# Attention scores of two heads on the two halves of the tensor engine's rows, with three products of parts

## The chip, the cores and the metric

One core of a Trainium2 chip runs the whole program. The metric is the device time of one execution in microseconds; several executions are timed and their median is given. Engines are called as in the profile: PE (TensorE, matmuls) and PEld (its loads of weights), DVE (VectorE), ACT (ScalarE), POOL (GpSimd), SP (SyncE, which issues most DMAs).

## What is computed

The reference is an encoder of two layers in float32 over 512 tokens and 1024 channels. Each layer has a mixer (windowed attention beside a gated short convolution) and a gated feed-forward network. The change lies in the scores of the attention. Cut to that part:

```python
N_HEADS, HEAD_DIM, N_KV_HEADS, GROUP, BLOCK, WINDOW = 16, 64, 4, 4, 128, 128

def one_block(args):
    qi, ki, vi, mi = args          # 128 queries, the three key blocks around them
    sc = jnp.einsum('bqkgd,bskd->bkgqs', qi.astype(jnp.float32), ki.astype(jnp.float32)) * scale
    sc = jnp.where(mi[None, None, None], sc, NEG_INF)
    m = jnp.maximum(jnp.max(sc, axis=-1, keepdims=True), sink_f)
    p = jnp.exp(sc - m)
    denom = jnp.sum(p, axis=-1, keepdims=True) + jnp.exp(sink_f - m)
    o = jnp.einsum('bkgqs,bskd->bqkgd', p / denom, vi.astype(jnp.float32))
    return o.astype(qi.dtype)
```

A score is a dot product over the 64 channels of a head. Four query heads share a key head. Tokens come in four blocks of 128; a query block sees its own key block and its neighbours, so the first and the last see two blocks (256 keys) and the two in the middle three (384 keys).

## The kernel before

All operands of a matmul are in the type fp32r, which keeps fewer bits than float32. So that little is lost, each operand is split into a high part, the value rounded to fp32r, and a low part, the rest. A projection (`mm3`, lines 182 to 184) adds up three products of parts: high by low, low by high, high by high. `split_to` (lines 213 and 214) makes the parts: one copy on ACT, one subtraction on DVE. A tile `u` from `unit` holds both parts of 128 rows by 512 tokens.

Activations lie transposed, channels on the 128 partitions and tokens along the free axis. `query_tile(n)` projects two query heads at a time: partitions 0 to 63 (`lo_p`) hold head 2n, partitions 64 to 127 (`hi_p`) head 2n + 1; `rope` rotates them on DVE. Then, in lines 685 to 687, the kernel before doesn't put high parts in one half of the tile and low parts in the other. For each of the two heads it writes a plane of 128 rows: the head's own 64 rows get its high part (ACT, line 686) and the other 64 rows its low part (DVE, line 687). `key_tile` writes, for each key head, a tile whose plane 0 is the high part on both halves of the partitions and whose plane 1 is the low part on both halves.

So one matmul over 128 rows adds two products of parts at once, and `scores` (line 708) needs two matmuls per head: against the low part of the keys and against the high part, all four products of parts together. The weights (the stationary operand) are 128 queries of a head, the moving operand 256 or 384 keys, and the sum lies in a PSUM bank of its own, which DVE reads on line 713 (scale, mask, maximum).

The unit of work is a key head `g` with a query block `b`: 16 units per layer. `scores(at, 0)` does heads 0 and 1 of the group, `scores(at, 2)` heads 2 and 3, so there are two blocks of four matmuls per unit and 64 blocks in the program. `softmax` follows on ACT and DVE, then `weights` (four transposes, line 742, and a split) and `values` (line 755) per key block. The generator `products` yields after every three matmuls of a projection, and the loop over `pieces` strews the attention's pieces among these projections: a block of scores comes after a few projections or right after the four transposes, and projections follow it. PE takes its instructions in this order. `bank` hands out eight PSUM banks in turn.

One more matmul matters for the prediction: on line 124, early in the program, the 48 rows of convolution taps are transposed by a matmul on 48 rows. All other matmuls of the kernel before have 128 rows.

Of the kernel before, what the change touches and what calls it, by code (L numbers as in the profile page):

```python
# [10 lines left out]
F32 = mybir.dt.float32  # L11
# [3 lines left out]
ALU = mybir.AluOpType  # L15

P = 128
# [51 lines left out]
def encoder(ctx: ExitStack, tc: tile.TileContext, a, out):  # L69
    nc = tc.nc  # L70
# [14 lines left out]
    def nm(s):  # L85
        names[s] = names.get(s, -1) + 1
        return f"{s}_{names[s]}"

    def bank():
        return pp.tile([P, 512], F32, tag="bank", name=nm("bank"))  # L90

    def unit(shape, dtype=F32R):
        return up.tile(shape, dtype, tag="u4", bufs=22, name=nm("u4"))

    def t4(shape, dtype=F32):
        return sp.tile(shape, dtype, tag="t4", bufs=6, name=nm("t4"))
# [4 lines left out]
    def small(n, s="sm"):  # L101
        return sp.tile([P, n], F32, tag=s, bufs=4, name=nm(s))
# [83 lines left out]
    def gemm_steps(w, c0, xs):  # L186

        hl = w_cols(w, c0)
        acc = bank()
        for k in range(KT):  # L190
            mm3(acc, hl(0, k), hl(1, k), xs(k, 0), xs(k, 1), k == 0, k == KT - 1)
            yield
        return acc
# [18 lines left out]
    def split_to(h, lo, src):  # L212
        nc.scalar.copy(h, src)
        nc.vector.tensor_tensor(out=lo, in0=src, in1=h.bitcast(F32), op=ALU.subtract)  # L214
# [346 lines left out]
    g = t4([P, D])  # L561
# [5 lines left out]
    for l in range(DEPTH):  # L567
# [4 lines left out]
        def rope(acc):  # L572
            r1, r2 = t2([P, T]), t2([P, T])
            nc.vector.stream_shuffle(r2, acc, SWAP)
            nc.vector.tensor_tensor(out=r1, in0=acc, in1=cos, op=ALU.mult)
            nc.vector.tensor_tensor(out=r2, in0=r2, in1=sin, op=ALU.mult)
            nc.vector.tensor_tensor(out=r1, in0=r1, in1=r2, op=ALU.add)
            return r1

        lo_p, hi_p = slice(0, HD), slice(HD, P)  # L580
        kk = []
# [97 lines left out]
        qs = [None] * KT  # L679

        def query_tile(n):
            acc = yield from gemm_steps(w_in, Q0 + n * P, xs)
            qr = rope(acc)
            u = unit([P, 2, T])
            for i, (own, other) in enumerate(((lo_p, hi_p), (hi_p, lo_p))):
                nc.scalar.copy(u[own, i], qr[own])
                nc.vector.tensor_tensor(out=u[other, i], in0=qr[own], in1=u[own, i].bitcast(F32), op=ALU.subtract)
            qs[n] = u


        def blocks(b):
            return max(b - 1, 0), min(b + 1, NT - 1)

        def scores(at, i0):
            g, b = at["unit"]
            lo_b, hi_b = blocks(b)
            w = (hi_b - lo_b + 1) * P
            m0 = (lo_b - (b - 1)) * P
            if i0 == 0:
                at["m"] = small(GROUP, "m")  # L700
                at["p"] = []
            ps = t4([P, 2, 3 * P])
            m = at["m"]
            for i in (i0, i0 + 1):
                s = bank()
                q = qs[2 * g + i // 2][:, i % 2, b * P : (b + 1) * P]
                for part in range(2):
                    nc.tensor.matmul(  # L708
                        s[:, :w], q, kk[g][:, 1 - part, lo_b * P : lo_b * P + w], start=part == 0, stop=part == 1
                    )  # L710
                h = l * HEADS + GROUP * g + i
                p = ps[:, i % 2, :w]
                nc.vector.tensor_tensor_reduce(  # L713
                    out=p, in0=s[:, :w], in1=mask[:, m0 : m0 + w], scale=HD**-0.5,
                    scalar=sink[:, h : h + 1], op0=ALU.add, op1=ALU.max, accum_out=m[:, i : i + 1],
                )
                at["p"].append(p)
# [97 lines left out]
        def products():  # L815
            for c in range(KT):
                if 2 + c < KT:
                    yield from query_tile(2 + c)
                for i in range(3):
                    yield from conv_job(c, i)  # L820
            for m in range(KT):
                yield from conv_proj(m)


        units = [{"unit": (g, b)} for g in range(KV) for b in range(NT)]
        pieces = [[lambda: scores(units[0], 0)], [lambda: (scores(units[0], 2), softmax(units[0]))], [], [], []]
        behind = None
        for i, at in enumerate(units):
            lo_b, hi_b = blocks(at["unit"][1])
            ahead = units[i + 1] if i + 1 < len(units) else None  # L830
            for n in range(hi_b - lo_b + 1):
                first, second = [], []
                if behind:
                    second.append(lambda f=behind: values(*f))
                if ahead and n == 0:
                    first.append(lambda ahead=ahead: scores(ahead, 0))
                second.append(lambda at=at, n=n: weights(at, n))
                if ahead and n == 0:
                    second.append(lambda ahead=ahead: (scores(ahead, 2), softmax(ahead)))
                pieces += [first, second]  # L840
                behind = (at, n)
        pieces += [[], [lambda: values(*behind)]]

        for n in range(2):
            run(query_tile(n))
# [184 lines left out]
```

## Time and profile before

| | |
|---|---|
| median of 3 runs | 1653.22 us (1651.73 to 1653.52) |
| the profiled execution | 1652.12 us |
| its span, first to last instruction | 1650.3 us |
| PE busy | 1638.5 us, 10071 matmuls |
| PEld busy | 1473.4 us, 10071 loads |
| DVE, ACT busy | 1226.6 us, 936.1 us |
| matmuls of scores (line 708) | 256: 128 with 256 keys, 128 with 384 keys |

The busy time of an engine is the time in which at least one of its instructions runs. Matmuls overlap: the record of one with 512 columns is 0.39 us long while the next starts after 0.23 us. What a matmul costs in a stream is therefore read from start to start. Each matmul has a load of its weights (LDWEIGHTS, on PEld), which normally begins when the matmul before it starts. In a row of the timeline the columns are start, length, engine, line, operation, output and inputs, shape and count; several equal instructions in a row are merged.

### The profile page before, as it was taken

Reading aid. Unit: us, or ns where it says so; the run is one execution under the profiler, and the core shown is the slowest. Engines: PE = TensorE matmul, PEld = TensorE weight load, DVE = VectorE, ACT = ScalarE, POOL = GpSimd, SP = SyncE. Lnnn points to the kernel's source line nnn. Section 1 sums busy time; section 2 is a strip of 40 time slices with the busy share of each in tenths; the row PEclk is TensorE's granted clock in tenths of the full one; section 3 lists DMA queues with packets and bytes.
Section 4 is the critical chain, followed back from the end, with each engine's and each line's share of the span. In section 5 each row is a group of like instructions: output and inputs, shape, how many; then the busy total and the mean of one; then the engine's idle time right before and its main releaser. Section 6 shows DMA issues by size and latency. Waiting matters only on the chain.

```text
span 1650.3 us, 26580 instructions
## 1 busy us (share of the span) xinstructions
PE 1638.5 (99%) x10071; PEld 1473.4 (89%) x10071; DVE 1226.6 (74%) x2383; ACT 936.1 (57%) x1974; POOL 98.8 (6%) x146
## 2 busy tenths in 40 slices
PE   9999999999999999999999999999999999999998
PEld 8888888889989999988898888888998899999886
DVE  6988876649779988854469788766696898888442
ACT  5566666547657555553346676664576665556331
POOL 0000000000012100000000000000010211001000
PEclk9999999999999999999999999999999999999999
DMA  6322222345575334343423222223357643443332
GB/s 210 90 77 77 64 81 73 89 116 128 173 204 97 104 104 113 109 136 130 151 65 102 77 77 77 77 67 89 102 145 215 165 105 108 109 110 121 103 115 77
DMA packets 254625, 182.84 MB, mean 111 GB/s; under 512 B 6000, under 2 KB 237472, under 8 KB 254496
## 3 DMA queue, kind: packets, MB, share of 16 engines
q1 hardware_dynamic: 246240, 171.70, 35.3%
q0 software_dynamic: 7680, 8.39, 3.4%
q8 instruction: 79, 1.29, 0.3%
q10 hardware_dynamic: 576, 1.05, 0.2%
q14 instruction: 50, 0.41, 0.1%
HBM read 164.34 MB, written 8.39 MB: 105 GB/s over the span
## 4 chain that ended last, share of the span: by engine, by line
PE 66%; DVE 2%; DMA 1%; issue 1%; ACT 0%; POOL 0%; SPq 0%; POOLq 0%; DVEq 0%; ACTq 0%
PE bank L182 21%; PE bank L183 21%; PE bank L184 21%; PE bank L708 1%; PE bank L755 1%; DMA u<-in_w_up_dram 1%; PE bank L742 1%; DVE hl L132 1%; DVE t L441 0%; PE bank L373 0%; PE bank L251 0%; DVE t L271 0%; ACT t L235 0%; DVE h L214 0%; DVE t L243 0%
## 5 line engine op out<-in xcount | busy, mean ns | idle before, releaser
L182 PE MATMUL bank<-h,hl 128*128 128x256 f32 (+1 forms) x1536 | 494.1, 322 | 1.9 <-DVE h L214 1.9
L183 PE MATMUL bank<-h,hl 128*128 128x256 f32 (+1 forms) x1536 | 490.2, 319 | 0.0
L184 PE MATMUL bank<-h,hl 128*128 128x256 f32 (+1 forms) x1536 | 490.1, 319 | 0.0
L132 DVE TENSOR_TENSOR hl<-raw,hl 128x512 fp32r<-128x512 f32 x396 | 269.4, 691 | 169.7 <-ACT hl L131 168.2
L131 ACT CAST hl<-raw 128x512 fp32r<-128x512 f32 x396 | 241.7, 620 | 262.4 <-PE bank L184 221.3
L184 PEld LDWEIGHTS bank<-h,hl 128*128 128x128 f32 x1536 | 292.6, 190 | 20.8
L182 PEld LDWEIGHTS bank<-h,hl 128*128 128x128 f32 x1536 | 292.7, 191 | 20.6 <-DVE h L214 2.8
L183 PEld LDWEIGHTS bank<-h,hl 128*128 128x128 f32 x1536 | 292.8, 191 | 17.5
L182 PE MATMUL bank<-u,hl 128*128 128x256 f32 (+1 forms) x976 | 305.2, 313 | 0.6 <-DVE t L497 0.6
L184 PE MATMUL bank<-u,hl 128*128 128x256 f32 (+1 forms) x976 | 303.7, 311 | 0.0
L183 PE MATMUL bank<-u,hl 128*128 128x256 f32 (+1 forms) x976 | 303.6, 311 | 0.0
L132 DVE TENSOR_TENSOR hl<-t,hl 128x512 fp32r<-128x512 f32 x240 | 180.7, 759 | 22.4 <-ACT hl L131 20.9
L182 PEld LDWEIGHTS bank<-u,hl 128*128 128x128 f32 x976 | 186.2, 191 | 11.2 <-DVE t L497 1.4
L184 PEld LDWEIGHTS bank<-u,hl 128*128 128x128 f32 x976 | 186.2, 191 | 10.3
L183 PEld LDWEIGHTS bank<-u,hl 128*128 128x128 f32 x976 | 186.3, 191 | 9.5
L131 ACT CAST hl<-t 128x512 fp32r<-128x512 f32 x240 | 147.3, 620 | 67.4 <-DVE t L441 41.9
L182 PE MATMUL bank<-hl,u 128*128 128x512 f32 x304 | 118.3, 389 | 0.0
L183 PE MATMUL bank<-hl,u 128*128 128x512 f32 x304 | 118.3, 389 | 0.0
L184 PE MATMUL bank<-hl,u 128*128 128x512 f32 x304 | 118.3, 389 | 0.0
L728 ACT ACTIVATE t<-t,neg 128x256 f32<-128x256 f32 (+1 forms) x128 | 70.4, 552 | 21.1 <-DVE neg L723 20.8
L441 DVE TENSOR_TENSOR t<-t,raw 128x512 f32<-128x512 f32 x112 | 75.3, 683 | 1.0
L713 DVE CUSTOM_DVE_ANT_0 t<-bank,tab,sink 128x256 f32<-128x256 f32 (+1 forms) x128 | 65.7, 542 | 6.1 <-PE bank L708 5.9
(142 smaller groups left out, 2280.0 us busy)
## 6 DMA issues: line engine op xcount, KB each, us to landing
raw<-in_w_in_dram SPq DMA_DIRECT2D x88, 512.0 KB, 3.9
u<-in_w_up_dram SPq DMA_DIRECT2D x44, 512.0 KB, 6.4
raw<-in_w_down_dram SPq DMA_DIRECT2D x44, 512.0 KB, 3.6
raw<-in_w_gate_dram SPq DMA_DIRECT2D x40, 512.0 KB, 4.1
raw<-in_w_conv_proj_dram SPq DMA_DIRECT2D x16, 512.0 KB, 3.6
raw<-in_w_attn_proj_dram SPq DMA_DIRECT2D x16, 512.0 KB, 3.6
u<-in_w_in_dram SPq DMA_DIRECT2D x16, 512.0 KB, 5.7
raw<-in_w_out_dram SPq DMA_DIRECT2D x16, 512.0 KB, 4.1
```

The source lines that it names most:

```text
L131: nc.scalar.copy(h, raw)
L132: eng.tensor_tensor(out=lo, in0=raw, in1=h.bitcast(F32), op=ALU.subtract)
L182: nc.tensor.matmul(acc, wh, xl, start=first, stop=False, skip_group_check=goes_on)
L183: nc.tensor.matmul(acc, wl, xh, start=False, stop=False, skip_group_check=goes_on)
L184: nc.tensor.matmul(acc, wh, xh, start=False, stop=last, skip_group_check=goes_on)
L441: add = lambda out, x, y: nc.vector.tensor_tensor(out=out, in0=x, in1=y, op=ALU.add)
L708: nc.tensor.matmul(s[:, :w], q, kk[g][:, 1 - part, lo_b * P : lo_b * P + w], start=part == 0, stop=part == 1)
L713: nc.vector.tensor_tensor_reduce(out=p, in0=s[:, :w], in1=mask[:, m0 : m0 + w], scale=HD**-0.5, scalar=sink[:, h : h + 1], op0=ALU.add, op ...
L728: nc.scalar.activation(p, p, AF.Exp, bias=neg[:, i : i + 1], accum_out=den[:, i : i + 1])
L742: nc.tensor.transpose(pt[:, i * P : (i + 1) * P], p[:, n * P : (n + 1) * P], ident)
L755: nc.tensor.matmul(o, v, hl[:, 1 - part], start=n == 0 and part == 0, stop=kb == hi_b and part == 1)
```

## The change

`query_tile` now splits both heads of a tile with one call of `split_to`: plane 0 holds the high parts of both heads on their own rows, plane 1 the low parts. `scores` takes two banks first and then goes through three products of parts: low queries by high keys, high by low, high by high. For each product it issues one matmul for the lower head on partitions 0 to 63 and one for the upper head on partitions 64 to 127. Each has 64 rows and 128 columns of weights. The product of the two low parts is no longer computed.

```diff
             acc = yield from gemm_steps(w_in, Q0 + n * P, xs)
             qr = rope(acc)
             u = unit([P, 2, T])
-            for i, (own, other) in enumerate(((lo_p, hi_p), (hi_p, lo_p))):
-                nc.scalar.copy(u[own, i], qr[own])
-                nc.vector.tensor_tensor(out=u[other, i], in0=qr[own], in1=u[own, i].bitcast(F32), op=ALU.subtract)
+            split_to(u[:, 0], u[:, 1], qr)
             qs[n] = u
...
             ps = t4([P, 2, 3 * P])
             m = at["m"]
-            for i in (i0, i0 + 1):
-                s = bank()
-                q = qs[2 * g + i // 2][:, i % 2, b * P : (b + 1) * P]
-                for part in range(2):
+
+            q = qs[2 * g + i0 // 2]
+            sums = [bank() for _ in range(2)]
+            for n, (a_part, b_part) in enumerate(((1, 0), (0, 1), (0, 0))):
+                for s, rows in zip(sums, (lo_p, hi_p)):
                     nc.tensor.matmul(
-                        s[:, :w], q, kk[g][:, 1 - part, lo_b * P : lo_b * P + w], start=part == 0, stop=part == 1
+                        s[:, :w], q[rows, a_part, b * P : (b + 1) * P], kk[g][rows, b_part, lo_b * P : lo_b * P + w],
+                        start=n == 0, stop=n == 2,
                     )
+            for i, s in zip((i0, i0 + 1), sums):
                 h = l * HEADS + GROUP * g + i
                 p = ps[:, i % 2, :w]
                 nc.vector.tensor_tensor_reduce(
```

Line 708 of the kernel before is line 707 of the changed one; lines after the scores move by one.

On PE the first block of scores, between two steps of a projection, reads in the kernel before (`u_2_480` holds the keys, `u_6_545` the queries; the shape is that of the output):

```order
L183 MATMUL bank_646<-h_86,hl_640 128x512
L184 MATMUL bank_646<-h_86,hl_640 128x512
L708 MATMUL bank_661<-u_2_480,u_6_545 128x256 x2
L708 MATMUL bank_665<-u_2_480,u_6_545 128x256 x2
L182 MATMUL bank_646<-h_86,hl_643 128x512
```

At the same place of the changed kernel:

```order
L183 MATMUL bank_640<-h_86,hl_634 128x512
L184 MATMUL bank_640<-h_86,hl_634 128x512
L707 MATMUL bank_655<-u_2_480,u_6_545 128x256
L707 MATMUL bank_656<-u_2_480,u_6_545 128x256
L707 MATMUL bank_655<-u_2_480,u_6_545 128x256
L707 MATMUL bank_656<-u_2_480,u_6_545 128x256
L707 MATMUL bank_655<-u_2_480,u_6_545 128x256
L707 MATMUL bank_656<-u_2_480,u_6_545 128x256
L182 MATMUL bank_640<-h_86,hl_637 128x512
```

Two pairs, each into one bank, have become six single matmuls that alternate between two banks. All 64 blocks change in this way, and every other matmul of PE keeps its place in the stream.

On DVE the two subtractions of a query tile, on 64 partitions each, stand in the kernel before like this, with the first reads of scores (line 713) behind the third tile's projection (`bank_602`):

```order
L687 TENSOR_TENSOR u_7_589<-t_10_583,u_7_589 64x512 x2
L574 STREAM_SHUFFLE t_13_628<-bank_602 128x512
L575 TENSOR_TENSOR t_12_627<-bank_602,tab 128x512
L576 TENSOR_TENSOR t_13_628<-t_13_628,tab 128x512
L713 ISA t_5_660,m_659<-bank_661,tab,sink 128x256
L713 ISA m_659 128x1
L577 TENSOR_TENSOR t_12_627<-t_12_627,t_13_628 128x512
L713 ISA t_5_660,m_659<-bank_665,tab,sink 128x256
```

In the changed kernel:

```order
L214 TENSOR_TENSOR u_7_587<-t_10_581,u_7_587 128x512
L574 STREAM_SHUFFLE t_13_624<-bank_598 128x512
L575 TENSOR_TENSOR t_12_623<-bank_598,tab 128x512
L576 TENSOR_TENSOR t_13_624<-t_13_624,tab 128x512
L132 TENSOR_TENSOR hl_753<-raw_748,hl_753 128x512
L577 TENSOR_TENSOR t_12_623<-t_12_623,t_13_624 128x512
L714 ISA t_5_654,m_653<-bank_655,tab,sink 128x256
L714 ISA m_653 128x1
L714 ISA t_5_654,m_653<-bank_656,tab,sink 128x256
```

One subtraction has taken the place of two, and the two reads of scores, which stood on either side of line 577's addition, now follow each other behind it.

## The prediction

> **What bounds the kernel now.** The page comes first: the share of busy time by engine, and the clock that the tensor engine was granted.
>
> ```profile
> span 1650.3 us, 26580 instructions
> ...
> PE 1638.5 (99%) x10071; PEld 1473.4 (89%) x10071; DVE 1226.6 (74%) x2383; ACT 936.1 (57%) x1974; POOL 98.8 (6%) x146
> ...
> PEclk9999999999999999999999999999999999999999
> ```
>
> PE holds a matmul in 99% of the span and its clock is full in every slice. A busy PE need not be a fast PE, since the ends of matmuls are modelled, so I read all its costs from one start to the next. The view of waits, for PE alone, is the second:
>
> ```profile
> PE bank L182 <- DVE h L214: 1.9, 2, 1.4
> PE bank L620 <- POOL ident masks.py:199: 1.4, 1, 1.4
> PE bank L251 <- DVE t L239: 1.2, 1, 1.2
> PE bank L182 <- DVE t L497: 0.6, 1, 0.6
> PE bank L183 <- DVE h L214: 0.5, 1, 0.5
> ```
>
> PE waits 5.6 us in all for other engines, and none of these waits is at a score, a transpose of weights or a value product. So the stage that the change touches is bound by PE's own stream: time that it gains or loses there goes to the span one for one. What the scores take comes from the groups of line 708 (shapes kept apart) and from the timeline of PE around one block of each width; the second column is the length, the first the start.
>
> ```profile
> L708 PE MATMUL bank<-u,u 128*128 128x384 f32 x128 | 29.0, 348 | 0.0
> ...
> L708 PE MATMUL bank<-u,u 128*128 128x256 f32 x128 | 21.5, 290 | 0.0
> ```
>
> ```profile
> 56.98 0.39 PE L184 MATMUL bank<-h,hl 128*128 128x512 f32 x1
> 57.20 0.64 PE L708 MATMUL bank<-u,u 128*128 128x256 f32 x4
> 57.67 0.40 PE L182 MATMUL bank<-h,hl 128*128 128x512 f32 x1
> ```
>
> ```profile
> 81.94 0.39 PE L184 MATMUL bank<-h,hl 128*128 128x512 f32 x1
> 82.16 0.87 PE L708 MATMUL bank<-u,u 128*128 128x384 f32 x4
> 82.87 0.40 PE L182 MATMUL bank<-h,hl 128*128 128x512 f32 x1
> ```
>
> 128 matmuls of each width in blocks of four are 32 blocks of each. A block of width 256 takes 57.67 - 57.20 = 0.47 us (0.12 a matmul), one of width 384 takes 82.87 - 82.16 = 0.71 us (0.18 a matmul). All scores together: 32 x (0.47 + 0.71) = 37.8 us, 2.3% of the span. That is all there is to save or multiply.
>
> **The change, part by part.**
>
> *Six matmuls for four.* Each block now has six matmuls on 64 rows instead of four on 128. Two neighbours use different halves of the array's rows, different banks, and neither needs the other. No row of this trace has two matmuls on separate rows, so the price is bounded from both sides. Lower end: the two halves run side by side and a block lasts three steps, 3 x 0.12 = 0.36 and 3 x 0.18 = 0.53 us; 32 x (0.11 + 0.18) = 9.3 us are gained. Upper end: they run one after the other, six steps, 0.71 and 1.07 us; 32 x (0.24 + 0.36) = 18.9 us (unrounded steps) are lost. I take the lower end: no wait, operand or bank joins the two, and what the trace shows of the array in one place speaks for it, since a weight load begins while the matmul before it still streams. But it is a choice, and both ends stay. The Trainium skill, "TensorE: Matmul & The Clock Gate", Part 3, says that matmuls on distinct row groups run concurrently and start some 4 ns apart; by that the sum would be the gain of 9.3 us, and no run here shows it yet.
>
> *The change of tile shape.* Every block now lies between matmuls on 128 rows. The program before does this once: the transpose of the conv taps on line 124 has 48 rows. It stands in the timeline of PE, and of the weight loads (PEld) for the same stretch:
>
> ```profile
> 31.76 0.28 PE L183 MATMUL bank<-hl,h 128*128 128x256 f32 x1
> 31.88 0.28 PE L184 MATMUL bank<-hl,h 128*128 128x256 f32 x1
> 32.09 0.26 PE L124 MATMUL bank<-ident,cw_rows 48*128 48x48 f32 x1
> 32.28 0.38 PE L182 MATMUL bank<-h,hl 128*128 128x256 f32 x1
> 32.50 0.28 PE L183 MATMUL bank<-h,hl 128*128 128x256 f32 x1
> ```
>
> ```profile
> 31.76 0.19 PEld L184 LDWEIGHTS bank<-hl,h 128*128 128x128 f32 x1
> 32.09 0.14 PEld L124 LDWEIGHTS bank<-ident,cw_rows 48*128 48x128 f32 x1
> 32.28 0.19 PEld L182 LDWEIGHTS bank<-h,hl 128*128 128x128 f32 x1
> 32.38 0.19 PEld L183 LDWEIGHTS bank<-h,hl 128*128 128x128 f32 x1
> ```
>
> Elsewhere the weights of a matmul are loaded one step ahead, when the one before it starts. Here neither L124's load nor the next L182's is early: each begins with its own matmul, after a gap. From L184's start at 31.88 to L183's at 32.50 are 0.62 us; L184 and L182 at their usual step (31.76 to 31.88) are 0.24 of it, so this trip to another shape cost 0.38 us, its one small matmul in it. The comparison is a trip to transposes of full size, eight in a row:
>
> ```profile
> 25.13 0.28 PE L183 MATMUL bank<-h,hl 128*128 128x256 f32 x1
> 25.25 0.28 PE L184 MATMUL bank<-h,hl 128*128 128x256 f32 x1
> 25.38 1.03 PE L251 MATMUL bank<-ident,t 128*128 128x128 f32 x8
> 26.16 0.36 PE L182 MATMUL bank<-hl,h 128*128 128x256 f32 x1
> 26.37 0.28 PE L183 MATMUL bank<-hl,h 128*128 128x256 f32 x1
> ```
>
> From 25.25 to 26.37 are 1.12 us; less 0.24, that is 0.88 for eight, 0.11 each and nothing left over. So neither the transpose nor the type costs the extra time, the shape does: 0.38 - 0.11 = 0.27 us if L124 itself is charged as a full transpose, 0.38 if as nothing. The semaphore that L124 waits for on PE is raised 82 matmuls earlier in the program, so a late input doesn't explain the gap. Other end: nothing per trip, if a single transpose on 48 rows says nothing of these matmuls. I take 0.38, since L124 has only 48 columns to stream and a score's weights, 32.38 - 32.28 = 0.10 us to load, must be loaded in the open on the way in and again on the way out. 64 blocks x 0.38 = 24.3 us lost; 64 x 0.27 = 17.3 us by the smaller figure. The Trainium skill, "TensorEngine Tiling (Array Packing)", Key Properties, has the rule that speaks against this change: switching the tiling mode drains the engine, moving between tiles of one mode does not. By that every block pays twice and its inner steps nothing, and the row of L124 agrees, with 0.38 us for the two.
>
> *The query split.* Per query tile two copies and two subtractions on 64 rows become one of each on 128.
>
> ```profile
> L687 DVE TENSOR_TENSOR u<-t,u 64x512 fp32r<-64x512 f32 x32 | 22.0, 686 | 1.7 <-ACT u L686 0.8
> ...
> L686 ACT CAST u<-t 64x512 fp32r<-64x512 f32 x32 | 19.8, 618 | 3.5 <-DVE t L577 3.1
> ```
>
> Half of each goes: 11.0 us on DVE and 9.9 us on ACT, since a subtraction on 128 rows (line 214) has the same free size. PE waits for neither, so I cost it at nothing. At most it is worth the 5.6 us that PE waits, and those are at other lines.
>
> *Banks and order.* Both banks are taken before the first score, so the second must be free one step of PE after the block's start instead of two, 0.12 us earlier. A bank that is late would hold up PE with the value products and projections queued behind it; the last column of L708's rows says 0.0 us idle, so today's banks are free in time, and eight of them rotate. DVE gets both banks about together at a block's end. It has room for that:
>
> ```profile
> core 0: us, PE busy (x) PEld busy (x) DVE busy (x) ACT busy (x) POOL busy (x), PEclk, DMA share, GB/s
> 50.00:150.00 100.00, 100.00 (x484) 83.90 (x483) 86.69 (x213) 63.94 (x152) 0.53 (x8) 1.00 0.31 90
> ```
>
> 87% busy in its fullest stretch before, and it loses 0.69 us per query tile there, while PE becomes slower. I cost this at nothing; without that cover it would be at most one subtraction (0.69 us) per unit of work, 32 x 0.69 = 22 us, but that needs DVE to be late in every unit. DMA (0.31) isn't near.
>
> **The sum.** -9.3 + 24.3 = +15.0 us. The profiled execution took 1652.1 us (its span and 1.8 us around it), so 1667.1; the median of the three runs lies 1.1 us above it, so 1668 us, 0.9% slower.
>
> **The rivals.**
>
> *A: forecast.* Halves side by side, a switch of shape per block. 1668, chance 0.38; with 0.27 per trip 1661.
>
> *B: weight loads set the pace.* Six loads per block instead of four. The loads above stand 0.10 us apart where they follow each other fastest, and the eight transposes, each with a load of its own, took 0.11 each. If loads for the two halves queue up behind each other at 0.11, the first and the last matmul of a block lie 5 x 0.11 = 0.55 us apart and a last step follows: 0.67 and 0.73 us, 32 x (0.20 + 0.02) = 7 us lost, and 24.3 for the switches: 1684. For it: no two loads in these rows start closer. Against it: all of those loads go to the same rows of the array. 0.22. The Trainium skill, "TensorE: Matmul & The Clock Gate", section LDWEIGHTS, has the time of a load go by its columns and not by its rows, so that 64 rows would load no faster; the loads of one type here all have 128 rows, so no row tells.
>
> *C: the halves take turns.* The change doesn't do what it says: each matmul waits for the one before, as every matmul of this trace does. 18.9 + 24.3 = 43 us: 1696. Nothing in the trace excludes it. 0.18.
>
> *D: faster.* Entering and leaving 64 rows is free for these matmuls and L124 was slow for reasons of its own (a 48-row load of another type). Then the gain stands alone: 1644. It decides at 9.3 / 64 = 0.145 us per trip: below that the change is a gain, above it a loss, with halves side by side. The one trip of the trace cost twice that. 0.12.
>
> *E: no switch, but no full overlap either* (B or C without the 24.3): 1660 to 1672, or as little as 1656 where loads overlap in part. 0.10.
>
> **The numbers.** About 0.2% (3.3 us) is what a measurement of this kernel can tell from no change. Slower by more: A, B, C and nearly all of E, 0.86. Within it: 0.03, a mixture of D and small switches. Faster: D, 0.11. The range goes from 1655 to 1697 and takes in A with either price of the trip, B, C and nearly all of E; D and dearer trips than L124's are left out, about 0.15.
>
> **What would show it.** Line 707 would have 384 matmuls with 64 rows. In a pair the second starts a few hundredths of a us after the first (A), one load later (B), or a full step of 0.12 or 0.18 later (C). Before the first of a block and before the first matmul after it, PE's start is late by some 0.2 us each, and the load starts with the matmul instead of a step ahead; if loads still run ahead across the border, D is right. The time from the first score to the projection after it would be some 0.55 and 0.72 us (three steps and the way out) for A; now it is 0.47 and 0.71. All else on PE keeps its steps, and DVE and ACT lose about 11 and 10 us of busy time. A new wait of PE for DVE at line 707, or steps that grow in the stages that the change doesn't touch, would make the working wrong whatever the total.

## The result, and the profile after

The changed kernel takes 1666.74 us (median of 4 runs, 1666.17 to 1667.69) against 1652.74 us for the kernel before on the same chip. The ratio is 1.0083 with a 95% interval from 1.0071 to 1.0095: slower by 13.7 us, between 11.7 and 15.7. The forecast was 1668, 15.0 us more than before.

The page of the changed kernel, as far as it answers to the lines of before, and its waits of PE:

```profile
span 1665.8 us, 26802 instructions
...
PE 1653.2 (99%) x10199; PEld 1461.0 (88%) x10199; DVE 1214.5 (73%) x2367; ACT 922.9 (55%) x1958; POOL 102.4 (6%) x146
...
PEclk9999999999999999999999999999999999999999
```

```profile
PE bank L251 <- DVE t L239: 2.2, 2, 1.2
PE bank L620 <- POOL ident masks.py:199: 1.4, 1, 1.4
PE bank L182 <- DVE h L214: 1.1, 2, 0.6
PE bank L182 <- DVE t L497: 0.8, 1, 0.8
PE bank L183 <- DVE h L214: 0.5, 1, 0.5
PE bank L182 <- ACT h L213: 0.2, 1, 0.2
```

The span grew by 15.5 us, PE's busy time by 14.7. DVE and ACT have 12 and 13 us less to do. PE still waits only some 6 us for others, and never at the scores (the new last row, 0.2 us, is at a projection). So the loss lies inside PE's stream. The timeline of PE around the first block of each width shows it:

```profile
56.66 0.39 PE L183 MATMUL bank<-h,hl 128*128 128x512 f32 x1
56.88 0.39 PE L184 MATMUL bank<-h,hl 128*128 128x512 f32 x1
57.20 0.62 PE L707 MATMUL bank<-u,u 64*128 64x256 f32 x6
57.75 0.50 PE L182 MATMUL bank<-h,hl 128*128 128x512 f32 x1
58.09 0.40 PE L183 MATMUL bank<-h,hl 128*128 128x512 f32 x1
```

```profile
69.84 0.39 PE L183 MATMUL bank<-h,hl 128*128 128x512 f32 x1
70.07 0.39 PE L184 MATMUL bank<-h,hl 128*128 128x512 f32 x1
70.39 0.79 PE L707 MATMUL bank<-u,u 64*128 64x384 f32 x6
71.10 0.50 PE L182 MATMUL bank<-h,hl 128*128 128x512 f32 x1
71.44 0.39 PE L183 MATMUL bank<-h,hl 128*128 128x512 f32 x1
```

Six matmuls now take 0.55 us from the first start to the projection behind them where four took 0.47, and 0.71 where four took 0.71. The rest of the loss stands beside the block: from L184 to the first score are 0.32 us instead of some 0.22, and from L182 to L183 behind the block 0.34 instead of 0.24. From the matmul ahead of a block to the second one behind it, a block of 256 keys takes 0.27 us more than before and one of 384 keys 0.21; over all 64 blocks of the two traces that is 15.5 us, the whole growth of the span. The loads of weights (PEld) in the same stretch say why:

```profile
56.66 0.19 PEld L184 LDWEIGHTS bank<-h,hl 128*128 128x128 f32 x1
57.20 0.41 PEld L707 LDWEIGHTS bank<-u,u 64*128 64x128 f32 x6 [0.35 <-issue]
57.75 0.19 PEld L182 LDWEIGHTS bank<-h,hl 128*128 128x128 f32 x1
57.86 0.19 PEld L183 LDWEIGHTS bank<-h,hl 128*128 128x128 f32 x1
```

L184's load began at 56.66, a step ahead of its matmul. The first score's load begins only with its matmul at 57.20, and so does L182's at 57.75: at both borders of the block nothing is loaded ahead. Inside a block, the counts of line 707's matmuls and loads in four stretches show the pairs (columns: stretch, length, PE busy and count, PEld busy and count, clock, DMA share, GB/s; an instruction counts in every stretch that it reaches into):

```profile
57.19:57.22 0.03, 0.02 (x2) 0.02 (x2) 1.00 1.07 324
57.19:57.41 0.22, 0.21 (x2) 0.21 (x4) 1.00 1.11 335
57.41:57.44 0.03, 0.03 (x4) 0.03 (x4) 1.00 1.01 307
57.53:57.56 0.03, 0.03 (x6) 0.03 (x2) 1.00 0.58 171
```

Two matmuls and two loads begin within 0.03 us, the loads of the next pair join them, and no third matmul starts before 57.41. The pairs begin at 57.20, 57.42 and 57.54, and L182 at 57.75: the second pair comes 0.22 us after the first instead of 0.12, and L182 0.20 after the third.

### The profile page after: what moved, and what is told of

The parts are those of the page before. It is cut to its first block, busy times and chain, and to the rows that moved or that the text cites. A ratio compares the mean times of both kernels' runs of the same rounds, so it can differ in the third digit from the quotient of the medians.

```text
span 1665.8 us, 26802 instructions
## 1 busy us (share of the span) xinstructions
PE 1653.2 (99%) x10199; PEld 1461.0 (88%) x10199; DVE 1214.5 (73%) x2367; ACT 922.9 (55%) x1958; POOL 102.4 (6%) x146
## 4 chain that ended last, share of the span: by engine, by line
PE 96%; DVE 1%; DMA 1%; ACT 1%; issue 0%; POOL 0%; SPq 0%; POOLq 0%; DVEq 0%; ACTq 0%
PE bank L182 30%; PE bank L183 29%; PE bank L184 29%; PE bank L707 2%; PE bank L756 2%; PE bank L743 2%; DMA u<-in_w_up_dram 1%; DMA raw<-in_w_in_dram 0%; PE bank L251 0%; DVE hl L132 0%; PE bank L373 0%; ACT t L235 0%; DVE t L441 0%; DVE t L271 0%; POOL r L229 0%
## 5 line engine op out<-in xcount | busy, mean ns | idle before, releaser
L182 PE MATMUL bank<-h,hl 128*128 128x256 f32 (+1 forms) x1536 | 500.1, 326 | 1.1 <-DVE h L214 1.1
L183 PE MATMUL bank<-h,hl 128*128 128x256 f32 (+1 forms) x1536 | 490.3, 319 | 0.0
L184 PE MATMUL bank<-h,hl 128*128 128x256 f32 (+1 forms) x1536 | 490.1, 319 | 0.0
L182 PEld LDWEIGHTS bank<-h,hl 128*128 128x128 f32 x1536 | 292.6, 190 | 30.3 <-issue 6.4
L184 PEld LDWEIGHTS bank<-h,hl 128*128 128x128 f32 x1536 | 292.6, 190 | 21.2
L183 PEld LDWEIGHTS bank<-h,hl 128*128 128x128 f32 x1536 | 292.9, 191 | 17.6
L182 PE MATMUL bank<-u,hl 128*128 128x256 f32 (+1 forms) x976 | 306.2, 314 | 0.9 <-DVE t L497 0.8
L184 PE MATMUL bank<-u,hl 128*128 128x256 f32 (+1 forms) x976 | 303.7, 311 | 0.0
L183 PE MATMUL bank<-u,hl 128*128 128x256 f32 (+1 forms) x976 | 303.5, 311 | 0.0
L182 PEld LDWEIGHTS bank<-u,hl 128*128 128x128 f32 x976 | 186.2, 191 | 13.3 <-DVE t L497 2.0
L184 PEld LDWEIGHTS bank<-u,hl 128*128 128x128 f32 x976 | 186.2, 191 | 10.3
L183 PEld LDWEIGHTS bank<-u,hl 128*128 128x128 f32 x976 | 186.3, 191 | 9.4
L183 PE MATMUL bank<-hl,u 128*128 128x512 f32 x304 | 118.3, 389 | 0.0
L182 PE MATMUL bank<-hl,u 128*128 128x512 f32 x304 | 118.3, 389 | 0.0
L184 PE MATMUL bank<-hl,u 128*128 128x512 f32 x304 | 118.3, 389 | 0.0
```

The source lines that it names most:

```text
L182: nc.tensor.matmul(acc, wh, xl, start=first, stop=False, skip_group_check=goes_on)
L183: nc.tensor.matmul(acc, wl, xh, start=False, stop=False, skip_group_check=goes_on)
L184: nc.tensor.matmul(acc, wh, xh, start=False, stop=last, skip_group_check=goes_on)
```

## The experiments

Each kernel was timed beside the kernel before on the same chip, where that one took 1652.3 to 1652.7 us; a ratio is to that time.

**Halves apart.** The changed kernel with the loops of a block exchanged:

```diff
-            for n, (a_part, b_part) in enumerate(((1, 0), (0, 1), (0, 0))):
-                for s, rows in zip(sums, (lo_p, hi_p)):
+            for s, rows in zip(sums, (lo_p, hi_p)):
+                for n, (a_part, b_part) in enumerate(((1, 0), (0, 1), (0, 0))):
```

> The changed kernel with the six matmuls of a block in another order: three on the lower half of the rows, then three on the upper half. Same matmuls, same banks, same trips to the 64-row shape, but only the third and the fourth matmul are neighbours on different halves. Theory (a trip costs 0.38 us, halves run side by side when neighbours): five steps per block instead of three, 32 x 2 x (0.12 + 0.175) = 18.9 us more than the changed kernel, 1685.6 us, and starts one step apart within a half. Rival (the starts of a pair are close, but the work behind them goes one after the other and a trip costs next to nothing, so that 18.9 us for six steps less a few give the loss that was seen): no difference from the changed kernel, 1666.7 us.

Measured: 1668.40 us, ratio to before 1.0092 (1.0074 to 1.0110), which can't be told from the changed kernel. The theory as written falls. Its first block in the timeline, and the counts of line 707 at its start:

```profile
56.95 0.39 PE L184 MATMUL bank<-h,hl 128*128 128x512 f32 x1
57.27 0.62 PE L707 MATMUL bank<-u,u 64*128 64x256 f32 x6
57.82 0.51 PE L182 MATMUL bank<-h,hl 128*128 128x512 f32 x1
```

```profile
57.26:57.29 0.03, 0.02 (x2) 0.03 (x2) 1.00 1.07 324
```

The block is as long as with the halves in turns, 0.55 us, and two matmuls again start at once, though the program lists three for one half first (the built program, too, has all three for the first bank ahead of the three for the second). Either the engine takes the fourth matmul ahead of the second and third, or pairing was never what made a block short. The next run decides.

**Both heads on one half.**

```diff
-                for s, rows in zip(sums, (lo_p, hi_p)):
+                for s, rows in zip(sums, (lo_p, lo_p)):
```

> The changed kernel with both heads' matmuls on the lower half of the rows, in the same order and into the same two banks. The second head's scores are then those of the first, so the output is not the reference's; count, sizes and trips are the same. Run because three matmuls on one half followed by three on the other cost nothing more. Theory (halves really work side by side, and the engine pairs them even when they are not neighbours): now nothing can be paired, six steps per block, 32 x 3 x (0.12 + 0.175) = 28 us more than the changed kernel, 1695 us (six steps of 0.71 and 1.07 us against three). Rival (pairs only start together in the records and their work was one after the other all along): no change, 1666.7 us.

Measured: 1695.35 us, ratio 1.0251 (1.0234 to 1.0268). Its first block:

```profile
58.43 0.39 PE L184 MATMUL bank<-h,hl 128*128 128x512 f32 x1
58.75 0.97 PE L707 MATMUL bank<-u,u 64*128 64x256 f32 x6
59.65 0.50 PE L182 MATMUL bank<-h,hl 128*128 128x512 f32 x1
```

0.90 us for six, against 0.55 with two halves, and the same 0.32 us ahead of it. So the halves do work side by side, and that is worth 28.6 us in this kernel; with halves apart the engine had really started matmuls out of the program's order.

**Trips alone, and their control.** Into the kernel before, ahead of the four matmuls of each block, goes one small matmul on 64 rows; the control has it on 128:

```diff
                 q = qs[2 * g + i // 2][:, i % 2, b * P : (b + 1) * P]
+                if i == i0:
+                    nc.tensor.matmul(s[:, :64], q[lo_p], kk[g][lo_p, 0, lo_b * P : lo_b * P + 64], start=True, stop=True)
```

```diff
+                    nc.tensor.matmul(s[:, :64], q, kk[g][:, 0, lo_b * P : lo_b * P + 64], start=True, stop=True)
```

> The kernel before, with one small matmul on 64 rows and 64 columns of keys put in front of the four of each block, into the same bank, which the next matmul overwrites: 64 trips to the other shape and nothing else changed. Theory: 64 x 0.38 = 24.3 us more than the kernel before, 1677.0 us, with the price of the small matmul in it. By the smaller figure of the working, 0.27 us plus a small matmul of some 0.05, 20.5 us: 1673. Rival (the shape is free and the small matmul counts as any other, at most a load of 0.11 us): up to 7 us, 1653 to 1660.

> The control of the kernel with trips alone (1679.4 us): the kernel before with the same small matmul in front of each block, 64 columns of keys, but on 128 rows, so with no change of shape. Theory (the shape costs the time, not the extra matmul): 64 x 0.03 to 0.11 us more than the kernel before, 1655 to 1660 us. Rival (any small matmul in front of a block costs that much, by its wait or its bank): 1679 us.

Measured: 1679.41 us with 64 rows, ratio 1.0163 (1.0144 to 1.0182), and 1659.83 us with 128, ratio 1.0038 (1.0023 to 1.0053). The first block of the one and of the other:

```profile
57.00 0.39 PE L184 MATMUL bank<-h,hl 128*128 128x512 f32 x1
57.32 0.29 PE L708 MATMUL bank<-u,u 64*128 64x64 f32 x1
57.54 0.74 PE L710 MATMUL bank<-u,u 128*128 128x256 f32 x4
58.12 0.40 PE L182 MATMUL bank<-h,hl 128*128 128x512 f32 x1
```

```profile
57.01 0.39 PE L184 MATMUL bank<-h,hl 128*128 128x512 f32 x1
57.24 0.19 PE L708 MATMUL bank<-u,u 128*128 128x64 f32 x1
57.27 0.72 PE L710 MATMUL bank<-u,u 128*128 128x256 f32 x4
57.83 0.40 PE L182 MATMUL bank<-h,hl 128*128 128x512 f32 x1
```

From L184 to L182 are 1.12 us with the trip and 0.82 without. The shape alone costs 0.30 us here, 19 us for 64 of them, and the whole trip with its matmul (1679.41 - 1652.46) / 64 = 0.42. The control lies at the upper end of what was expected, 0.11 us per small matmul, about the 0.10 to 0.11 us between two loads of weights; the rival, which put the whole cost on any small matmul, falls.

**One trip per unit.** Both blocks of a unit are put next to each other, twelve matmuls in a row (and likewise for the first unit, which stands ahead of the loop):

```diff
-                    first.append(lambda ahead=ahead: scores(ahead, 0))
+                    first.append(lambda ahead=ahead: (scores(ahead, 0), scores(ahead, 2)))
...
-                    second.append(lambda ahead=ahead: (scores(ahead, 2), softmax(ahead)))
+                    second.append(lambda ahead=ahead: softmax(ahead))
```

> The changed kernel with both blocks of a unit next to each other: twelve matmuls on 64 rows in one piece, 32 pieces instead of 64. The softmax stays where it was. Theory (the cost is paid on the way in and out of the shape): 32 trips fewer at 0.38 us, 12.2 us, so 1654.5 us, with no gap between the sixth and the seventh matmul. Rival (the cost goes by matmuls, loads of weights or banks): 1666.7 us, as the changed kernel. If four banks at once hold up PE, it shows as waits of PE at the scores and the time lies between.

Measured: 1654.67 us, ratio to before 1.0010 (1.0001 to 1.0019), 12.1 us under the changed kernel: 0.38 us for each of 32 trips saved. A block of twelve with 384 keys:

```profile
69.61 0.39 PE L184 MATMUL bank<-h,hl 128*128 128x512 f32 x1
69.93 1.33 PE L707 MATMUL bank<-u,u 64*128 64x384 f32 x12
71.18 0.50 PE L182 MATMUL bank<-h,hl 128*128 128x512 f32 x1
```

1.25 us for twelve, under twice the 0.71 us of six. Banks did not hold PE up: it waits 5.7 us in all, and not at the scores. What is left over the kernel before is 32 x 0.39 - 9.3 = 3.2 us by the numbers above, 2.2 measured (0.2 to 3.1).

**The query split alone**, in the kernel before:

```diff
-            for i, (own, other) in enumerate(((lo_p, hi_p), (hi_p, lo_p))):
-                nc.scalar.copy(u[own, i], qr[own])
-                nc.vector.tensor_tensor(out=u[other, i], in0=qr[own], in1=u[own, i].bitcast(F32), op=ALU.subtract)
+            split_to(u[:, 0], u[:, 1], qr)
```

> The kernel before with the query split of the change alone: one copy and one subtraction on 128 rows per query tile. The matmuls of the scores stay as they were, two of 128 rows per head on the planes of the tile, and therefore mix two heads: the scores are not those of the reference, the work on PE is the same. Theory (DVE and ACT are covered by PE): no change, 1652.7 us, with some 11 and 10 us less busy time on DVE and ACT. Rival (part of the split is on the path): up to 5.6 us faster, all that PE waits, 1647.

Measured: 1653.25 us, ratio 1.0002 (0.9993 to 1.0011).

```profile
PE 1638.7 (99%) x10071; PEld 1473.1 (89%) x10071; DVE 1212.6 (73%) x2367; ACT 922.3 (56%) x1958; POOL 98.6 (6%) x146
```

14 us less on DVE and on ACT, where 11 and 10 were expected, and no change of the time: both are covered by PE.

**How far the engine looks ahead.** Three orders of the twelve matmuls of a unit, in the kernel with one trip per unit. `scores` takes four banks and does the four heads at once; `i` is the head and `n` the product of parts:

```diff
+            lower = [(i, n) for i in (0, 2) for n in range(3)]
+            upper = [(i, n) for i in (1, 3) for n in range(3)]
+            for i, n in lower[:4] + upper + lower[4:]:
```

This is the order four, six, two. The first of the three kernels has all of `lower` and then all of `upper`, the last has 5 in the place of 4.

> The kernel with one trip per unit, with its twelve matmuls in the order six on the lower half, then six on the upper half. Theory (the two halves take their matmuls independently of the order in which the program lists them): paired from the start, 1654.7 us as with lower and upper in turns. Rival (the engine looks only a few matmuls ahead, three being near the limit): the upper half starts late, up to six steps more per unit, 16 x 6 x (0.12 + 0.175) = 28 us, 1683 us, or something between that tells how far it looks.

> One trip per unit again, with the order four matmuls on the lower half, six on the upper, two on the lower. In the kernel with six and six the first matmul of the upper half started with the fourth of the lower, so three steps late, and three lower ones stood ahead of it then; with three and three it started at once. Theory (the engine finds a matmul for the idle half when no more than three with their loads stand ahead of it): one step late here, seven steps per unit instead of six, 16 x (0.12 + 0.175) = 4.7 us more than the 1654.7 us of lower and upper in turns, 1659.4 us. Rival (the upper half waited there for its banks or its operands, not for its place in the order): three steps late again, as with six and six, 1666.8 us; or at once, 1654.7 us.

> One trip per unit, order five on the lower half, six on the upper, one on the lower. Four ahead turned out to cost nothing: with the first of them begun, three with their loads stood ahead of the first upper one, so that the limit of three was right and its use on four was wrong by one. Theory (three waiting matmuls with their loads may stand ahead, no more): here four wait when the first begins, so the upper half is let in when the second lower matmul has begun and runs from the third on, two steps late: 16 x 2 x (0.12 + 0.175) = 9.4 us, or two thirds of the 12.1 us of six and six, 8 us: 1662 to 1664 us, the same in all 32 units. Rival (the limit lies elsewhere, or six and six was held up by its order of banks): at once, 1654.4 us, or three steps late, 1666.8 us.

Measured: six and six 1666.77 us (ratio 1.0082, 1.0067 to 1.0097); four, six, two 1654.39 (1.0011, 1.0002 to 1.0021); five, six, one 1662.32 (1.0057, 1.0041 to 1.0074). The first units, one fence for each in that order:

```profile
57.26 1.32 PE L706 MATMUL bank<-u,u 64*128 64x256 f32 x12
58.50 0.50 PE L182 MATMUL bank<-h,hl 128*128 128x512 f32 x1
```

```profile
57.26 0.99 PE L708 MATMUL bank<-u,u 64*128 64x256 f32 x12
58.18 0.50 PE L182 MATMUL bank<-h,hl 128*128 128x512 f32 x1
```

```profile
57.29 1.20 PE L708 MATMUL bank<-u,u 64*128 64x256 f32 x12
58.42 0.50 PE L182 MATMUL bank<-h,hl 128*128 128x512 f32 x1
```

Twelve matmuls with 256 keys take 0.92 us when four of the lower half stand first, 1.13 with five and 1.24 with six. The counts at the start of six and six show the lower half alone for two matmuls, and the upper half coming in with the third (in the last stretch the first two still run):

```profile
57.25:57.35 0.10, 0.10 (x1) 0.10 (x1) 1.00 1.07 317
57.35:57.59 0.24, 0.24 (x2) 0.24 (x3) 1.00 0.89 265
57.59:57.62 0.03, 0.03 (x4) 0.03 (x3) 1.00 0.45 137
```

With five first it comes in with the second, at 57.52:

```profile
57.50:57.53 0.03, 0.03 (x3) 0.03 (x3) 1.00 0.38 103
```

In all 32 units of these two kernels it is so. Two expectations had the place wrong: with six and six the upper half starts with the third lower matmul and not the fourth, and with five first with the second (0.22 us, or two steps, behind the first). The expectation for four, six, two was a step off: with the first matmul begun, only three still wait ahead of the first upper one. Counted so, all four orders (three and three among them) agree: a matmul for the idle half is started when no more than three others with their loads, not yet begun, stand ahead of it. The banks are the same four in the three kernels, so they don't explain the difference.

## Why the prediction was right

*PE's stream is the bound.* Right: PE waits 6.2 us for others against 5.6, nothing of it at the scores, and the 64 blocks account for the growth of the span.

*Halves side by side, a block of three steps.* Right, and the choice that was least supported by the trace of before: a load that begins under a running matmul says nothing of two matmuls side by side, so that this end and not the other came true was partly luck. Pairs start within 0.03 us, and one half alone costs 28.6 us more. The Trainium skill, "TensorE: Matmul & The Clock Gate", Part 3, has distinct row groups run concurrently, and here the trace agrees. The reason given, that neighbours share nothing, was too narrow: they need not be neighbours.

*A trip of 0.38 us.* Right: 0.10 on the way in, 0.11 on the way out and 0.19 or 0.18 inside the block (0.55 less three steps of 0.12, 0.71 less three of 0.18) are 0.40 and 0.39. Twelve matmuls in one trip saved 0.38 per trip. The parts were not quite as forecast: the first score is late by 0.10 us and not by some 0.2, and as much again lies between the first pair and the second. The single transpose on line 124 gave the price of 64 blocks, but only by the choice to charge its matmul at nothing. The smaller figure of 0.27 is near what trips alone cost over their control, 0.30. That a block costs 0.09 us more than that fits the late second pair, which a trip with one matmul doesn't have; no run takes this apart, and part of the agreement on 0.38 may be luck. The Trainium skill, "TensorEngine Tiling (Array Packing)", Key Properties, calls a switch of the mode a drain; that fits the late loads at both borders and twelve matmuls in one trip at less than twice the time of six.

*The sum.* -9.3 + 64 x 0.39 = 15.7 us against 15.5 between the two profiled spans; the medians lie 14.0 us apart, and the forecast was 15.0.

*The split and the banks at nothing.* Right: the split alone leaves the time as it was, and no wait of PE appeared at line 707.

Rival B falls on the loads: two begin at once and cost nothing more, though a load on 64 rows is hardly shorter (0.18 us) than one on 128 (0.19). Rival C forecast 1696 for matmuls one after the other; the kernel with both heads on one half is just that and took 1695.35, and the changed kernel is 28.6 us below it. D and E fall on trips alone, where the shape costs 0.30 us, twice the 0.145 at which D and A part.

## What to carry to other kernels

Matmuls on half the rows do run in pairs, but each stay in that shape is paid on the way in and out, here some 0.39 us, as much as three matmuls of 256 columns; count the stays before the gain per stay (0.11 to 0.18 us for six instead of four). By these numbers work on half rows pays only where more of it stands together, which no run shows: one stay per unit was still 2.2 us behind the kernel before, and more units in one stay, of which two would take all eight PSUM banks, were not tried. A single odd instruction in the old trace, with its neighbours' starts, can give the price of something the program hardly does, within the bounds of how its own work is charged (here 0.27 to 0.38 us).

## What the runs showed of the hardware

The tensor engine doesn't start matmuls on different row halves in the program's order. With three and three it ran them as pairs (1668.4 us, as in turns), with four first at no cost, with five and six first at 8 and 12 us. That PE takes its instructions in their order, as is said of the kernel before, thus holds there, where all scores have 128 rows. The Trainium skill, "TensorE: Matmul & The Clock Gate", Part 3, says that matmuls start and end strictly in program order; the starts in these runs don't when their rows differ, and the measurement decides.

The signals of completion did keep the order. With five, six, one the last matmul listed is on the lower half, and in all 32 units it starts 0.23 to 0.28 us before the last upper one, and its record ends as much earlier. Its semaphore nevertheless rises only 0.02 to 0.05 us after the end of the upper one's record. So here a wait for the last matmul listed did cover the others.

Loads of weights for the two halves also begin together (two within 0.03 us), whereas loads for the same rows never came closer than 0.10 us in the rows shown. Four pairs of transposes' loads in the trace of before do, at 0.06 us.
